# adaLN steps moved out of the first head pair of a neighbourhood-attention stage

## The chip, the cores and the metric

The kernel runs on one core of a Trainium2 chip. The time is device microseconds of one execution; a run is the median of several. The engines are TensorE (PE; PEld is its weight load), VectorE (DVE), ScalarE (ACT), GpSimd (POOL) and SyncE (SP), which here only issues DMAs.

## The reference, cut to what matters

Two layers over 512 latent and 256 context tokens of width 1024: a gated linear attention layer and a neighbourhood attention layer, each followed by a gated MLP with a width-3 convolution. Every sub-layer is RMSNorm, adaLN (a shift and a scale), mixer, gate, residual. The neighbourhood layer, for 16 heads of 64:

```python
mod_l = (sc_lat @ ada_w[i] + ada_b[i])[:, None, :]
sh1_l, s1_l, g1_l, sh2_l, s2_l, g2_l = jnp.split(mod_l, 6, axis=-1)
h_l = modulate(x_lat, norm1_g[i], sh1_l, s1_l)
s_nb = jnp.einsum('bchd,bicjhd->bhcij', q_r, k_win)      # 8 x 16 window of latent keys
s_nb = s_nb + bias[None]                                 # learned, by relative place
s_cx = jnp.einsum('bchd,blhd->bhcl', q_r, k_c)           # all 256 context keys
p = jax.nn.softmax(jnp.concatenate([s_nb, s_cx], axis=-1), axis=-1)
o = p_nb @ v_win + p_cx @ v_c
x_lat = x_lat + g1_l * (o @ w_out)
```

The second layer's MLP uses sh2, s2 and g2 of the same `mod_l`; the context's output is not needed any more.

## The kernel before, in words

**Order of the work.** The program is written with a tile framework. The source gives an order of instructions; a planner then orders each engine's queue, by its own estimate of what is ready when, the earlier in the source first among the ready ones. At run time each engine works its queue strictly in that order, and a wait holds everything behind it on the same engine. SP's queue of DMA issues is such a queue too. A tile pool's memory goes to the next pool when the old pool's users are done.

**Matmuls.** Every weight tile of 128 x 1024 comes by DMA into a `st` tile (three buffers) and is split into a high part (`wh`, ACT, L283) and a rest (`wl`, DVE, L284); a product is three matmuls (`mm3`, L288 to L290). The split weights live in a ring that holds five such tiles.

**Last step of the MLP before.** `last_outs` (L1053) adds the outputs to the residual and runs the next norm along with them, first for the latents, then for the context. The norm's temporary tiles come from `scratch`: `tt`, which is one buffer and listed twice, and four big tiles (3h, 3l, 4h, 4l), in the order tt, 3h, 3l, tt, 4h, 4l. All lie in the pool `ffn0`, whose memory the neighbourhood stage's pool `na` takes over. A norm step writes `hh` (ACT) and `hl` (DVE).

**The neighbourhood stage** goes over eight pairs of heads. For pair `pr` the queries, keys and values were projected during pair `pr - 1` (`proj`, with weights that `weights` loads and splits). The latents are in 4 tiles of 128 tokens. For each tile `t`: `scores(pr, t)` does the score matmuls (L1207), then for each of the two heads DVE adds the bias and takes the row maximum (L1214, `mx`), POOL negates it (L1217, `ng`), ACT takes the exponential and its sum (L1219), DVE the reciprocal (L1221, `ri`), POOL scales the row (L1222, `S`). `turn(pr, t)` transposes the probabilities on PE (L1232) and copies them to `PT`, one head by ACT (L1235), one by DVE (L1237). `values(pr, t)` multiplies with the values (L1249). Between these stand the projections for the next pair, and for odd pairs from 3 on the output projection of two earlier pairs (`out_group`, added to the residual by DVE, L312).

**Bias.** `raw` holds a pair's learned bias, `nmask` two masks (inner and edge), both loaded at the start of the stage, L1126 and L1130. POOL fills the tiles `bias0` and `bias1` with constants and adds raw and mask into their first and last quarter and a half (L1145, four additions per head). Tile 0 reads columns 256 to 768 (edge), the others columns 0 to 512 (inner).

**adaLN.** Four vectors of 1024 (gate 1, shift 2, scale 2, gate 2 of the second layer) are computed on DVE meanwhile: `ada_lanes` makes 33 jobs, one that starts two loads and 8 steps for each vector. A step multiplies a 128 x 1024 tile `sa` with a column and accumulates in `acc` (L206 for the first, L208 for the others), and issues the load for the step after next (L198); `sa` has two buffers. The eighth step also sums `acc` over partitions on PE (L214), turns the result and adds its bias. Each pair takes four jobs from the list, at four places between its scores and transposes.

Of the kernel before, what the change touches and what calls it, by code (L numbers as in the profile page):

```python
# [13 lines left out]
OP = mybir.AluOpType  # L14
# [25 lines left out]
def body(ctx, tc, x, ctx_x, small, ada0, ada, w_gla, a_w1, a_w2, w_go, w_fi, w_fo,  # L40
         w_nqk, w_no, rpb, ident_d, rope_d, lvl_d, nmask_d, *outs):
    nc = tc.nc
# [372 lines left out]
    with tc.tile_pool(name="gla", bufs=6) as pool:  # L415
# [342 lines left out]
        for h in range(HEADS):  # L758
            part_a(h, turn_early if h == HEADS - 1 else None)
            n = h + 1  # L760
# [76 lines left out]
    def ffn0():  # L837
# [3 lines left out]
        with tc.tile_pool(name="ffn0", bufs=1) as pool:  # L841
            def big(i, e, dt=FR):
                return pool.tile([128, 4 * HT], dt, name=f"T{i}{e}", tag=f"T{i}{e}")

            def scratch(tags):

                n = [0]

                def new(name):
                    n[0] += 1  # L850
                    tg = tags[n[0] % len(tags)]
                    if tg == "tt":
                        return pool.tile([128, T + 1], F32, name=name, tag="tt")[:, 0:512]
                    return big(*tg, F32)[:, 0:512]

                return new
# [10 lines left out]
            tmp = scratch([(i, e) for i in (4, 2) for e in "hl"])  # L867
# [96 lines left out]
            def weights_a(j):  # L964

                s_ = st[j] = {"a": wload(w_fi[0, j, 0])}
                s_["A"] = wsplit(s_["a"])
# [15 lines left out]
            def weights_c(j):  # L983
                st[j]["S4"], st[j]["A22"] = (wsplit(t_)[0] for t_ in st[j]["left"])

            def first(j):
                s_ = st[j]
                s_["b1"], s_["b2"] = ps_aux(), ps_mm()
                product(s_["b1"], s_["A"][0], 11, True)
                s_["s1"] = copied(s_["b1"])  # L990
                product(s_["b2"], s_["A"][1], 21, True)
# [27 lines left out]
            def lane():  # L1019
                if jobs:  # L1020
                    jobs.pop(0)()

            jobs = ada_lanes([(1, m, c) for m in range(2) for c in range(2)],
                             lambda: ast.tile([128, 1024], F32, name="acc", tag="sa"),
                             lambda: pool.tile([128, HT], F32, name="rows", tag="cp", bufs=5)[:, 0:256], 1)
# [4 lines left out]
            for grp in GROUPS:  # L1030
                for j in grp:
                    if j < 2:
                        continue
                    if j < NF - 1:
                        weights_a(j + 1)
                    weights_c(j)
                    if j < NF - 1:
                        first(j + 1)
                    us[j] = final_(j)
                    if j < NF - 1:  # L1040
                        to_pad(j + 1)
                        weights_b(j + 1)
                        middle(j + 1)
                ul = [us[j] for j in grp]
                n = len(grp)
                w = [h for j in grp for h in wsplit(wload(w_fo[0, j]))]

                def block(i):
                    return lambda d: tuple(t_[:, d % 4 * 128:d % 4 * 128 + 128] for t_ in w[d // 4 * n + i])

                ws = [block(i) for i in range(n)]
                if grp is GROUPS[-1]:
                    last_outs(0, ws, ul, 0, (LAT, CTX),  # L1053
                              lambda rng: Norm(pool, 1, 0, rng, blocks=rng == LAT, acc=apad[:, rng[0]:rng[1]],
                                               tmp=scratch(["tt", (3, "h"), (3, "l"), "tt", (4, "h"), (4, "l")])))
                    continue
                for d in range(KD):
                    for rng in (LAT, CTX):
                        add_gated(ffn_out(ws, ul, d, rng, 0), 0, 1, d, rng)
# [60 lines left out]
    with tc.tile_pool(name="na", bufs=5) as pool:  # L1120
# [6 lines left out]

        load_raw(0)
        nmask = pool.tile([128, 2, 256], F32, name="nmask", bufs=1)
        nc.sync.dma_start(nmask, nmask_d.rearrange("v p n -> p v n"))  # L1130
        biasT = [pool.tile([128, 768], F32, name=f"bias{i}", bufs=1) for i in range(2)]
        for bt in biasT:
            nc.gpsimd.memset(bt, 0.0)
# [1 line left out]
                nc.gpsimd.memset(bt[0:64, o + 192:o + 256], NEG)  # L1135
                nc.gpsimd.memset(bt[64:128, o:o + 64], NEG)

        def load_bias(hd):
            bt = biasT[hd % 2]
            rv = raws[hd // 2][:, hd % 2, :]  # L1140
            for var, o in ((0, 0), (1, 512)):
                for half in range(2):
                    ps_ = slice(64 * half, 64 * half + 64)
                    o2 = o + 64 * half
                    nc.gpsimd.tensor_tensor(bt[ps_, o2:o2 + 192], rv[ps_], nmask[ps_, var, 64 * half:64 * half + 192],  # L1145
                                            OP.add)
            return bt

        biases = {0: [load_bias(hh) for hh in range(2)]}
        sp = [dict() for _ in range(8)]  # L1150

        def weights(pr, i):
            sp[pr]["w", i] = tuple(w.rearrange("p (k n) -> p k n", k=KD) for w in wunit(w_nqk[pr, i]))
# [46 lines left out]
        def scores(pr, t):  # L1200
            qe, ke = sp[pr][0], sp[pr][1]
            pss = [ps_aux() for _ in range(2)]
            for off, ks in ((W0[t], slice(128 * t, 128 * t + 256)), (C0[t], slice(640, 896))):
                for i, (a_, b_) in enumerate(((1, 0), (0, 1), (0, 0))):
                    for hh in range(2):
                        p_ = slice(64 * hh, 64 * hh + 64)
                        mm(pss[hh][:, off:off + 256], qe[a_][p_, 128 * t:128 * t + 128], ke[b_][p_, ks],  # L1207
                           start=i == 0, stop=i == 2)
            S2 = res.tile([128, D], F32, name="S2", tag="xc", bufs=2)
            for hh in range(2):  # L1210
                S = S2[:, hh * 512:hh * 512 + 512]
                mx = sml.tile([128, 1], F32, name="mx", tag="mx")
                bt = biases[pr][hh]
                nc.vector.tensor_tensor_reduce(S, pss[hh], bt[:, 0:512] if t else bt[:, 256:768], 1.0, -3.0e38,  # L1214
                                               OP.add, OP.max, mx)
                ng = sml.tile([128, 1], F32, name="ng", tag="ng")
                nc.gpsimd.tensor_scalar(ng, mx, -1.0, 0.0, OP.mult, OP.add)  # L1217
                sm = sml.tile([128, 1], F32, name="sm", tag="sm")
                nc.scalar.activation(S, S, AF.Exp, bias=ng, accum_out=sm)  # L1219
                ri = sml.tile([128, 1], F32, name="ri", tag="ri")  # L1220
                nc.vector.reciprocal(ri, sm)  # L1221
                nc.gpsimd.tensor_scalar(S, S, ri, 1.0, OP.mult, OP.mult)  # L1222
            sp[pr]["S", t] = S2

# [47 lines left out]
        def out_groups(m, t0, t1):  # L1272
            for d in range(2 * t0, 2 * t1):
                out_group(m, d)

        jobs = ada_lanes([(1, m, 0) for m in range(2, 6)],
                         lambda: pool.tile([128, 1024], F32, name="acc", tag="acc", bufs=1),
                         lambda: pool.tile([128, 256], F32, name="rows", bufs=1), 2)
        jobs.pop(0)()
        for i in range(3):  # L1280
            weights(0, i)
        for i in range(3):
# [5 lines left out]
        for pr in range(8):  # L1288
            nx = pr + 1
            more = nx < 8  # L1290
            m = (pr - 3) // 2
            outs_now = pr >= 3 and pr % 2 == 1
            if more:
                for i in range(3):
                    weights(nx, i)
            if outs_now:
                out_weights(m)
            if more:
                load_raw(nx)
            scores(pr, 0)  # L1300
            if pr:
                values(pr - 1, 3)
            if more:
                proj(nx, 0, LAT)
            scores(pr, 1)
            if more:
                proj(nx, 1, LAT)
            elif outs_now:
                out_groups(m, 0, 1)
            jobs.pop(0)()  # L1310
            turn(pr, 0)
            scores(pr, 2)
            jobs.pop(0)()
            values(pr, 0)
            if more:
                proj(nx, 1, CTX)
                proj(nx, 2, CTX)
                v_turn(nx, CTX)
            if outs_now:
                out_groups(m, 1 - more, 2)  # L1320
            turn(pr, 1)
            scores(pr, 3)
            jobs.pop(0)()
            values(pr, 1)
            if more:
                biases[nx] = [load_bias(2 * nx + hh) for hh in range(2)]
                proj(nx, 2, LAT)
            turn(pr, 2)
            jobs.pop(0)()
            if outs_now:  # L1330
                out_group(m, 4)
                if more:
                    out_group(m, 5)
            if more:
                v_turn(nx, LAT)
            values(pr, 2)
            turn(pr, 3)
            if outs_now and more:
                out_groups(m, 3, 4)
# [118 lines left out]
```

## Time and profile before

| | |
|---|---|
| median of 3 runs | 1719.58 us (1718.56 to 1719.92) |
| profiled execution | 1717.33 us |
| its span, first to last instruction | 1715.5 us |
| PE busy | 1647.6 us, 96% |
| DVE busy | 1188.4 us, 69% |
| ACT busy | 740.0 us, 43% |
| POOL busy | 205.8 us, 12% |
| share of PE in the chain that ended last | 73% |
| neighbourhood stage | about 994 to 1318 us of the span |

A busy PE is not PE at its peak, as matmuls overlap; what counts is where it stops, for whom, and at which granted clock. All times in the rows are from the span's start.

### The profile page before, as it was taken

The numbers are of one execution on the slowest core, as the hardware profiler recorded it, in microseconds if no ns is written. First come the engines' busy times: TensorE is split into PE (matmuls) and PEld (weight loads), VectorE is DVE, ScalarE is ACT, GpSimd is POOL, SyncE is SP. The second block draws the span as 40 slices with busy tenths as digits, with TensorE's granted clock in tenths as the row PEclk, the third lists the DMA queues.
The fourth block names the chain that finished last, engine by engine and source line by source line (L and its number), as shares of the span: only waits on it lengthen the run. The fifth ranks groups of instructions, "written<-read, shape, count | busy, mean of one in ns | idle before, by whom it ended". The sixth has DMA issues, their size and how long they took to land.

```text
span 1715.5 us, 27141 instructions
## 1 busy us (share of the span) xinstructions
PE 1647.6 (96%) x10867; PEld 1413.3 (82%) x10867; DVE 1188.4 (69%) x1973; ACT 740.0 (43%) x1331; POOL 205.8 (12%) x321
## 2 busy tenths in 40 slices
PE   5999999999999999999999989999999999999997
PEld 3768778777899999999999768887877888888887
DVE  4797877875998877978767774647476755555555
ACT  3665756663753342433434544433334522222332
POOL 1031222320000000000000042423231000000000
PEclk9999999999999999999999989999999999999999
DMA  7653423013333332524223151414141232322321
GB/s 270 182 173 106 166 75 105 20 50 136 98 122 112 116 106 75 172 67 143 98 63 110 27 191 54 141 47 161 41 135 38 85 96 90 99 89 84 110 86 50
DMA packets 54190, 179.70 MB, mean 105 GB/s; under 512 B 7024, under 2 KB 10864, under 8 KB 54064
## 3 DMA queue, kind: packets, MB, share of 16 engines
q1 hardware_dynamic: 54064, 177.97, 32.4%
q8 instruction: 85, 1.39, 0.3%
q14 instruction: 41, 0.34, 0.1%
HBM read 173.75 MB, written 2.10 MB: 103 GB/s over the span
## 4 chain that ended last, share of the span: by engine, by line
PE 73%; DVE 11%; ACT 5%; issue 4%; POOL 3%; DMA 3%; SPq 0%; POOLq 0%; DVEq 0%; ACTq 0%
PE mm L288 14%; PE mm L289 14%; PE mm L290 14%; PE aux L288 8%; PE aux L289 8%; PE aux L290 8%; PE mm L1249 1%; DMA sa<-in 1%; PE aux L1232 1%; POOL bias L1145 1%; DVE t L571 1%; DVE acc L208 1%; PE aux L650 1%; PE aux L1207 1%; PE aux L615 1%
## 5 line engine op out<-in xcount | busy, mean ns | idle before, releaser
L288 PE MATMUL mm<-hh,wl 128*128 128x512 f32 (+3 forms) x864 | 308.1, 359 | 5.0 <-ACT hh L372 2.5
L289 PE MATMUL mm<-hl,wh 128*128 128x512 f32 (+3 forms) x864 | 302.9, 351 | 0.0
L290 PE MATMUL mm<-hh,wh 128*128 128x512 f32 (+3 forms) x864 | 302.4, 351 | 0.0
L289 PE MATMUL mm<-ul,wh 128*128 128x512 f32 (+1 forms) x544 | 188.7, 347 | 0.2 <-DVE ul L301 0.2
L288 PE MATMUL mm<-uh,wl 128*128 128x512 f32 (+1 forms) x544 | 188.9, 349 | 0.0
L290 PE MATMUL mm<-uh,wh 128*128 128x512 f32 (+1 forms) x544 | 188.7, 348 | 0.0
L288 PEld LDWEIGHTS mm<-hh,wl 128*128 128x128 f32 (+1 forms) x864 | 163.7, 190 | 29.0 <-issue 5.3
L312 DVE SCALAR_TENSOR_TENSOR xl<-mm,mod,xl 128x512 f32<-128x512 f32 (+1 forms) x168 | 116.2, 698 | 94.4 <-PE mm L290 93.8
L283 ACT ACTIVATE wh<-st 128x1024 fp32r<-128x1024 f32 (+1 forms) x127 | 131.8, 1051 | 113.5 <-issue 69.6
L290 PEld LDWEIGHTS mm<-hh,wh 128*128 128x128 f32 (+1 forms) x864 | 164.0, 190 | 18.0 <-issue 0.4
L289 PEld LDWEIGHTS mm<-hl,wh 128*128 128x128 f32 (+1 forms) x864 | 164.1, 190 | 17.7 <-issue 1.0
L288 PE MATMUL aux<-hh,wl 128*128 128x384 f32 (+2 forms) x496 | 173.9, 351 | 0.0
L289 PE MATMUL aux<-hl,wh 128*128 128x384 f32 (+2 forms) x496 | 173.5, 350 | 0.0
L290 PE MATMUL aux<-hh,wh 128*128 128x384 f32 (+2 forms) x496 | 173.4, 350 | 0.0
L284 DVE TENSOR_TENSOR wl<-st,wh 128x1024 fp32r<-128x1024 f32 (+1 forms) x126 | 153.8, 1226 | 22.5 <-ACT wh L283 22.1
L263 ACT ACTIVATE wh<-st 128x512 fp32r<-128x512 f32 (+1 forms) x126 | 94.1, 756 | 165.0 <-issue 57.0
L348 POOL TENSOR_TENSOR rs<-ms,mhalf 128x2 f32<-128x2 f32 (+1 forms) x10 | 10.9, 1094 | 932.2 <-DVE ms L346 932.2
L288 PEld LDWEIGHTS mm<-uh,wl 128*128 128x128 f32 x544 | 102.4, 189 | 15.9 <-ACT uh L300 2.0
L289 PEld LDWEIGHTS mm<-ul,wh 128*128 128x128 f32 x544 | 102.5, 188 | 15.0 <-DVE ul L301 0.6
L264 DVE TENSOR_TENSOR wl<-st,wh 128x512 fp32r<-128x512 f32 (+1 forms) x126 | 104.6, 849 | 13.6 <-ACT wh L263 13.0
L290 PEld LDWEIGHTS mm<-uh,wh 128*128 128x128 f32 x544 | 102.4, 188 | 13.2
L288 PEld LDWEIGHTS aux<-hh,wl 128*128 128x128 f32 x496 | 93.6, 189 | 8.5 <-issue 1.2
(330 smaller groups left out, 3251.3 us busy)
## 6 DMA issues: line engine op xcount, KB each, us to landing
st<-in SPq DMA_DIRECT2D x201, 512.0 KB, 3.7
sa<-in SPq DMA_DIRECT2D x98, 512.0 KB, 4.2
sx<-in SPq DMA_DIRECT2D x14, 512.0 KB, 6.1
xl<-in SPq DMA_DIRECT2D x8, 512.0 KB, 6.2
xc<-in SPq DMA_DIRECT2D x4, 512.0 KB, 8.2
out<-y SPq DMA_DIRECT2D x16, 128.0 KB, 1.7
raw<-in SPq DMA_DIRECT2D x16, 96.0 KB, 2.4
t<-q SPq DMA_DIRECT2D x16, 64.0 KB, 2.5
```

Source lines behind the costliest of these rows:

```text
L208: nc.vector.scalar_tensor_tensor(acc[0], st, cs[:, k, c:c + 1], acc[0], OP.mult, OP.add)
L263: nc.scalar.activation(hi, s_, AF.Copy)
L264: nc.vector.tensor_sub(lo, s_, hi.bitcast(F32))
L283: nc.scalar.activation(hi, st, AF.Copy)
L284: (eng or nc.vector).tensor_sub(lo, st, hi.bitcast(F32))
L288: mm(out, a[1], b[0], start=first, stop=False, **at)
L289: mm(out, a[0], b[1], start=False, stop=False, **at)
L290: mm(out, a[0], b[0], start=False, stop=last, **at)
L312: nc.vector.scalar_tensor_tensor(x_, ps, gate(l, n, d, rng), x_, OP.mult, OP.add)
L571: nc.vector.tensor_mul(ek, ek, st[h]["k"])
L615: mm(ps[:, 0:DV], st[h]["kt", d][:, c * CH:(c + 1) * CH], st[h]["v", c], start=True, stop=True)
L650: mm(ps[:, 0:DV], a_, b_, start=i == 0, stop=i == len(terms) - 1)
```

## The change

The neighbourhood stage takes no adaLN job in pair 0; pairs 1 to 4 take five, pairs 5 to 7 four. Each job's DVE instructions are queued on DVE behind the last softmax reciprocal written before it (`tc.issue_after` fixes the order on one engine's queue and adds no wait for an end). The weight loads of the next pairs are queued on SP behind the load of the mask. The bias additions go edge first, both heads, then inner, both heads. The norm at the end of the MLP before no longer uses `tt` as a scratch tile.

```diff
-                                               tmp=scratch(["tt", (3, "h"), (3, "l"), "tt", (4, "h"), (4, "l")])))
+                                               tmp=scratch([(3, "h"), (3, "l"), (4, "h"), (4, "l")])))
...
-        nc.sync.dma_start(nmask, nmask_d.rearrange("v p n -> p v n"))
+        mask_load = nc.sync.dma_start(nmask, nmask_d.rearrange("v p n -> p v n"))
...
-        def load_bias(hd):
-            bt = biasT[hd % 2]
+        def bias_part(hd, var, o):
             rv = raws[hd // 2][:, hd % 2, :]
-            for var, o in ((0, 0), (1, 512)):
-                for half in range(2):
...
+        def load_biases(pr):
+            for var, o in ((1, 512), (0, 0)):
+                for hh in range(2):
+                    bias_part(2 * pr + hh, var, o)
...
-                nc.vector.reciprocal(ri, sm)
+                anchor[0] = nc.vector.reciprocal(ri, sm).ins
...
+        def lane(pr, fifth=False):
+            if pr and (pr < 5 or not fifth):
+                with tc.issue_after(anchor[0]):
+                    jobs.pop(0)()
...
             if more:
-                for i in range(3):
-                    weights(nx, i)
+                with tc.issue_after(mask_load.ins):
+                    for i in range(3):
+                        weights(nx, i)
...
                 proj(nx, 0, LAT)
+            lane(pr, fifth=True)
             scores(pr, 1)
...
-            jobs.pop(0)()
+            lane(pr)
             turn(pr, 0)
             scores(pr, 2)
-            jobs.pop(0)()
+            lane(pr)
             values(pr, 0)
...
             scores(pr, 3)
-            jobs.pop(0)()
+            lane(pr)
             values(pr, 1)
             if more:
-                biases[nx] = [load_bias(2 * nx + hh) for hh in range(2)]
+                load_biases(nx)
                 proj(nx, 2, LAT)
             turn(pr, 2)
-            jobs.pop(0)()
+            lane(pr)
```

## Rows read from the trace of the kernel before

**Rows 1.** Waits of PE, first pair, 1002 to 1036 (total us, times, longest).

```profile
PE mm L1249 <- DVE PT L1237: 2.5, 1, 2.5
PE mm L1249 <- ACT PT L1235: 2.3, 1, 2.3
...
PE aux L1232 <- POOL S L1222: 0.9, 1, 0.9
```

**Rows 2.** Waits of PE, later pairs, 1036 to 1320.

```profile
PE mm L1249 <- DVE PT L1237: 3.8, 3, 2.1
```

**Rows 3.** Timeline of PE, first pair (start, duration, instruction, count).

```profile
1014.45 0.60 PE L1232 MATMUL aux<-ident,S 128*128 128x128 f32 x4
...
1026.56 0.58 PE L288 MATMUL mm<-hh,wl 128*128 128x256 f32 x1
...
1030.55 0.28 PE L288 MATMUL mm<-hh,wl 128*128 128x256 f32 x1
...
1034.13 0.40 PE L288 MATMUL mm<-hh,wl 128*128 128x512 f32 x1
...
1035.10 1.04 PE L1232 MATMUL aux<-ident,S 128*128 128x128 f32 x8
...
1038.00 0.50 PE L288 MATMUL mm<-hh,wl 128*128 128x512 f32 x1
```

**Rows 4.** Stretches: us; busy PE, PEld, DVE, ACT, POOL; granted clock, DMA share, GB/s.

```profile
1020.50:1026.50 6.00, 2.52 (x16) 1.85 (x16) 5.58 (x9) 1.75 (x6) 2.11 (x3) 0.50 0.69 207
1026.50:1030.50 4.00, 4.00 (x19) 3.94 (x19) 0.41 (x4) 1.31 (x4) 1.57 (x3) 0.50 0.23 91
```

**Rows 5.** Timeline of DVE, first pair (idle before, and what ended it, in brackets).

```profile
1013.78 1.28 DVE L208 SCALAR_TENSOR_TENSOR acc<-sa,cs,acc 128x1024 f32<-128x1024 f32 x1 [4.47 <-DMA sa<-in]
...
1020.90 2.91 DVE L208 SCALAR_TENSOR_TENSOR acc<-sa,cs,acc 128x1024 f32<-128x1024 f32 x2
...
1023.94 0.68 DVE L1237 COPY PT<-aux 128x512 f32<-128x512 f32 x1
```

**Rows 6.** Stretches, adaLN accumulation alone: busy PE, PEld, DVE; clock, DMA share, GB/s.

```profile
993.00:1030.00 37.00, 0.00 (x0) 0.00 (x0) 10.93 (x8) 0.87 0.61 194
1030.00:1079.00 49.00, 0.00 (x0) 0.00 (x0) 0.00 (x0) 0.99 0.16 52
...
1243.00:1272.00 29.00, 0.64 (x8) 0.16 (x8) 10.47 (x8) 1.00 0.58 181
```

**Rows 7.** Timeline of POOL, first pair.

```profile
1000.12 7.21 POOL L1145 TENSOR_TENSOR bias<-raw,nmask 64x192 f32<-64x192 f32 x8 [2.89 <-DMA nmask<-in]
...
1011.31 0.70 POOL L1222 TENSOR_SCALAR S<-S,ri 128x512 f32<-128x512 f32 x1
...
1021.08 1.66 POOL L1222 TENSOR_SCALAR S<-S,ri 128x512 f32<-128x512 f32 x1 [0.33 <-DVE ri L1221]
```

**Rows 8.** Timeline of DVE, seventh pair.

```profile
1268.84 1.29 DVE L208 SCALAR_TENSOR_TENSOR acc<-sa,cs,acc 128x1024 f32<-128x1024 f32 x1 [0.63 <-DMA sa<-in]
```

**Rows 9.** DMA issues (KB, us to landing): whole page, then 993 to 1003.

```profile
st<-in SPq DMA_DIRECT2D x201, 512.0 KB, 3.7
...
nmask<-in SPq DMA_DIRECT2D x1, 256.0 KB, 4.9
```

**Rows 10.** Timeline of SP's DMA queue, 970 to 1012.

```profile
977.93 15.86 SPq L247 DMA_DIRECT2D st<-in  x5
993.89 1.17 SPq L1126 DMA_DIRECT2D raw<-in  x2
995.11 0.58 SPq L1130 DMA_DIRECT2D nmask<-in  x1
```

**Rows 11.** Timeline of DVE, end of the norm before the stage.

```profile
992.17 1.22 DVE L284 TENSOR_TENSOR wl<-st,wh 128x1024 fp32r<-128x1024 f32 x1
993.31 0.48 DVE L373 SCALAR_TENSOR_TENSOR hl<-hf,mod,hh 128x256 fp32r<-128x256 f32 x1
```

**Rows 12.** Timeline of PE, entry of the stage.

```profile
994.76 0.39 PE L288 MATMUL mm<-hh,wl 128*128 128x256 f32 x1 [1.39 <-ACT v L1171]
```

More of the change, by code (lines that the diff above doesn't have):

```diff
@@ L1136, in body @@
                 nc.gpsimd.memset(bt[64:128, o:o + 64], NEG)
-        def load_bias(hd):
-            bt = biasT[hd % 2]
+        def bias_part(hd, var, o):
             rv = raws[hd // 2][:, hd % 2, :]
-            for var, o in ((0, 0), (1, 512)):
-                for half in range(2):
[L1143 to L1149, printed above, removed]
+            for half in range(2):
+                ps_ = slice(64 * half, 64 * half + 64)
+                o2 = o + 64 * half
+                nc.gpsimd.tensor_tensor(biasT[hd % 2][ps_, o2:o2 + 192], rv[ps_],
+                                        nmask[ps_, var, 64 * half:64 * half + 192], OP.add)
+        def load_biases(pr):
+            for var, o in ((1, 512), (0, 0)):
+                for hh in range(2):
+                    bias_part(2 * pr + hh, var, o)
+        load_biases(0)
         sp = [dict() for _ in range(8)]
@@ L1212, in scores @@
                 mx = sml.tile([128, 1], F32, name="mx", tag="mx")
-                bt = biases[pr][hh]
+                bt = biasT[hh]
                 nc.vector.tensor_tensor_reduce(S, pss[hh], bt[:, 0:512] if t else bt[:, 256:768], 1.0, -3.0e38,
@@ L1279, in body @@
         jobs.pop(0)()
+        anchor = [None]
+        def lane(pr, fifth=False):
+            if pr and (pr < 5 or not fifth):
+                with tc.issue_after(anchor[0]):
+                    jobs.pop(0)()
         for i in range(3):
```

## The prediction

> **What bounds the kernel now.** The order of reading: who TensorE (PE) waited for, the PE timeline where it waited, then the queue that kept it waiting. In the neighbourhood stage (about 994 to 1318 us of the span) PE nearly always has matmuls, so only its stops are worth time. With the first pair of heads it stopped for both copies of the transposed probabilities, 2.5 and 2.3 us [rows 1]; for all seven later pairs together it waited 3.8 us for such a copy [rows 2]. So the stage has one bad place and three small ones.
>
> The bad place: the transposes of the first pair start at 1014.45, and the next projection, which needs nothing from them, only at 1026.56 because PE works in order behind them [rows 3]. From 1020.5 to 1030.5 the granted clock is 0.50, the lower level, 1.2 GHz, after PE had begun to stop [rows 4].
>
> Why: VectorE (DVE) also works in order. The adaLN accumulation of 1013.78 starts after 4.47 us in which DVE sat idle for that step's DMA; the second head's reciprocal and all later softmax work stand behind it. At 1020.90 two more accumulations (2.91 us) stand ahead of the PT copy of 1023.94 [rows 5]. The code asks for four adaLN jobs per pair, but the planner issues what it thinks ready: all 8 steps of a vector come in one burst (8 in 993 to 1030, none in 1030 to 1079, 8 again in 1243 to 1272) [rows 6]. A burst runs as fast as 512 KB loads land, and softmax shares its queue.
>
> **Part 1: no adaLN step with the first pair.** From the table of jobs: before 8 pairs x 4 = 32 steps; after 0 + 4 x 5 + 3 x 4 = 32. Nothing is removed but the place. Time without stops, from the same pair's second round: transposes at 1035.10, scores, values, next projection at 1038.00, so 2.90 us for the three [rows 3]. From 1014.45 that gives 1017.35 in place of 1026.56: 9.21 us. Then the clock: 18 matmuls of 256 columns took 1026.56 to 1030.55, 3.99 us; the next 30 took 3.58 us (to 1034.13), 0.12 each [rows 3], so 18 cost 2.16: another 1.83 us. Sum 11.04. I take 0.3 off for a remaining wait on a PT copy: **10.7 us**. What is late next? The softmax must be ready at 1014.45 without the accumulations: its POOL work waited behind eight bias additions (1000.12, 7.21 us) and even so the first scaling ran at 1011.31 [rows 7]; the second head's would follow by about 0.7. Cover: the two projections that PE runs until 1014.45. Their weights must then be there (part 3).
>
> **Part 2: later steps pinned behind a softmax's reciprocal.** The 32 steps (about 1.3 us each, 10.2 to 10.9 us for eight [rows 6]) can't run early in bursts any more; each follows the last reciprocal traced before it. Queued behind a pinned step: PT and V copies, key and query splits, the next softmax. Gain: the 3.8 us of [rows 2], where a step with a late load (1268.84, 0.63 idle and 1.29 us) stands just ahead of a PT copy [rows 8]. With one step per softmax two loads are always in flight a softmax apart, longer than the 4.9 us that a load took in a crowd [rows 9]. Bounds: all 3.8 won; or, if a step still lands ahead of each of those three copies, 1.29 lost at each, -3.9. The pin's reason and the free DVE time between bursts put me near the first: **3.0 us**. The fifth jobs in pairs 1 to 4 add 4 x 1.3 = 5.2 us of DVE to stretches that hold no accumulation now [rows 6]: nothing on the path while spread, and 1.29 apiece if ahead of a copy (inside the bound above).
>
> **Part 3: mask, raw bias and the weights of pair 1.** SP issued five weight loads from 977.93 on, then raw at 993.89 and mask at 995.11 [rows 10]. Raw starts 0.1 us after the last `hl` of the context norm ends (993.31 + 0.48), and that norm is the last user of the previous pool [rows 11]. So mask and raw wait for the pool, not for SP, and taking `tt` out of the scratch list cannot by itself release them: the same last norm step writes another tile of that pool. What can: pair 1's weight loads now stand behind the mask, so their two DVE splits (like that of 992.17, 1.22 us, 1.14 until the next starts) no longer stand among the norm's steps. That moves the release to about 993.8 - 2.3 = 991.5, mask to 992.7. PE's idle 1.39 us at 994.76, waiting for the evacuation that waits for the same release [rows 12], may go too: gain 0 to 1.4. Price: pair 1's first weights are issued after the mask, at about 993.4 instead of 977.93; plus 3.7 (median landing) to 4.9 us [rows 9], plus the two halves of a split, about 2.3 (each near the 1.22 of the DVE half): usable 999.4 to 1000.6, or up to 2.3 us later if the release isn't earlier (1002.9). PE takes them after two context projections of 24 matmuls (48 x 0.12 = 5.8 us) and the first scores (about 1.5, half of the 2.90 above): 994.76 + 7.3 = 1002.1, or 1000.7 if the 1.4 is gained. So between -1.5 and +1.4 us; the nearest case is just in time: **+0.6 us gained**.
>
> Scratch of four tiles for one `tt` and four: every step now waits for the fourth before it, instead of `tt` for the third. DVE was busy nearly without a break there, so I count 0, bounds -1.0 to +0.5 (one norm step of 0.48 us, late twice, or early once). Edge biases first: pair 0's first softmax needs four of the eight additions, 3.6 of 7.21 us; nothing waits for it before 1014.45, so 0 now; if the mask came late they are the cover.
>
> **Sum**: 10.7 + 3.0 + 0.6 = 14.3 us. The profiled execution took 1717.33 us, 1.8 around its span of 1715.5; it becomes 1703.0. The median of the runs is 2.25 above the profiled one: 1719.58 - 14.3 = **1705.3 us**.
>
> **A rule against the change.** POOL's scaling of the probabilities took 0.70 us at 1011.31 and 1.66 at 1021.08, where it started just after an accumulation [rows 5, 7]. The pin puts every accumulation right behind the reciprocal that releases such a scaling. The Trainium skill (SBUF — State Buffer, Who interferes with whom) says that a DVE instruction with two SBUF inputs and a GpSimd instruction that reads SBUF exclude each other for the whole instruction, whoever starts first. By that rule, and the trace agrees with it here, each scaling beside a step would be about 1 us later; the sum would be unchanged as long as PE has a projection between softmax and transposes.
>
> **Rivals.**
> A. The stall only moves: part 1 comes, part 2 doesn't, and pairs 2, 4 and 6 keep their stops or trade them for others of 1.29 us per step; entrance 0. For it: DVE is dense there. Against: only three steps must miss a copy. 10.7 - 2.0 = 8.7 gained (between 10.7 and 6.8): **1710.9**.
> B. Mask no sooner, weights of pair 1 late (the part that doesn't do what it says). The pool is released at 993.8 still; weights usable 1002.9 to 1005 (the second of them a step behind the first), PE stops 1 to 3 us before its projection and may fall to the lower clock for another 1.8, as in the first pair. 10.7 + 3.0 - 4.8 = 8.9: **1710.7**. For it: the release is by the last norm step in both kernels.
> C. No change: the first pair's stop is not DVE's. If, with accumulations gone, the PT copies were as late, only part 2's 3 us would come and the weights' delay would eat them: **1719**. Against it: the 4.47 us idle is named DMA of `sa`, and that DMA is gone.
> D. Slower: the collision of scaling and accumulation reaches PE. Place: POOL's scaling after each pinned step; price 1.66 - 0.70 = 0.96 us each; up to 32 steps, 31 us. It cancels the gain from 14.3 / 0.96 = 15 steps on; at 25 of 32 (24 us): 1719.58 - 14.3 + 24 = **1729**. Against it: PE waited for a scaling once, 0.9 us, and inside the bad place [rows 1]; between any scores and their transposes stand at least two groups of projection, as from 1002 to 1014.45.
>
> **How the numbers follow.** Forecast 0.62 (own range 1701.5 to 1709), A 0.13, B 0.12, C 0.07, D 0.06. 0.2% (3.4 us) is about what a measurement of this kernel can tell from no change. Forecast, A and B are faster: 0.87, with a little of C's lower side against a little of A's upper one. C is the same: 0.07. D slower: 0.06. The range reaches from 1701.5 (all of 11.0, 3.8, 1.4 and 0.5, and the 1.4 by which the runs shown differ) to 1713 (A and B with their worse ends), leaving out C, D and thin tails.
>
> **What would show it.** Right: no accumulation before about 1040; the transposes of the first pair followed without a stop by scores, values and projection at about 1016 to 1018; granted clock 1.00 through 1014 to 1034; one accumulation behind each second reciprocal afterwards; the waits for PT in later pairs under 1 us. Part 3 right: mask issued at about 992.7 and no PE stop at the first pair-1 projection; wrong: mask still near 994 or PE waiting for `wl` at about 1001. The prediction is wrong if the first pair still stops PE for more than 3 us, or if scalings beside accumulations are what PE's transposes wait for.

## The result, and the profile after

The changed kernel takes **1704.18 us**, median of 5 runs (1703.84 to 1705.13), against 1719.58 (1718.56 to 1720.27, 5 runs): a ratio of 0.9910, 95% interval [0.9899, 0.9921]. That is 15.4 us faster; forecast were 14.3 and 1705.3 us. The profiled execution took 1703.84 us, its span 1702.1. Of the five executions behind run 8's 1702.91 us below, one took 5473.84 us at a granted clock of 0.269, and it is the profiled one, so no row of that run is shown.

Who PE waited for, 1002 to 1320 of the changed kernel, the window of [rows 1, 2] together (total us, times, longest):

```profile
PE mm L288 <- DVE xl L312: 2.0, 1, 2.0
PE mm L288 <- DVE wl L284: 1.7, 1, 1.7
PE mm L288 <- ACT oh L300: 0.9, 1, 0.9
PE mm L1252 <- DVE PT L1240: 0.7, 1, 0.7
PE aux L214 <- DVE acc L208: 0.5, 1, 0.5
```

The lines after L1055 have moved by a few (L1249 is L1252 now, L1237 is L1240, L1222 is L1225). Both waits of [rows 1] for copies of PT are gone, and so are the three of [rows 2]. The 0.7 us for PT are new: they stand in pair 7, behind a pinned step, where before no accumulation ran (PE and DVE after; accumulations alone before):

```profile
1285.00 1.09 PE L1252 MATMUL mm<-PT,V 128*64 128x128 f32 x14 [0.69 <-DVE PT L1240]
```

```profile
1283.08 1.26 DVE L208 SCALAR_TENSOR_TENSOR acc<-sa,cs,acc 128x1024 f32<-128x1024 f32 x1
```

```profile
1272.00:1318.00 46.00, 0.64 (x8) 0.16 (x8) 0.00 (x0) 1.00 0.08 24
```

The wait for `wl` is new too (part 3 below); the two for `xl` and `oh` lie at the stage's end and were there before (1.7 and 0.7 us).

The first pair on PE, in answer to [rows 3] (start, duration, instruction, count):

```profile
1015.60 1.03 PE L1235 MATMUL aux<-ident,S 128*128 128x128 f32 x8
...
1016.56 0.39 PE L1210 MATMUL aux<-kh,ql 64*128 64x256 f32 x2
...
1017.47 1.09 PE L1252 MATMUL mm<-PT,V 128*64 128x128 f32 x16
1018.49 0.39 PE L288 MATMUL mm<-hh,wl 128*128 128x256 f32 x1
```

Transposes, scores, values, next projection, without a stop: 2.89 us from 1015.60 to 1018.49, where before it took 12.11 (1014.45 to 1026.56). The stretches, in answer to [rows 4] (us; busy PE, PEld, DVE, ACT, POOL; granted clock, DMA share, GB/s):

```profile
1015.60:1021.00 5.40, 5.40 (x58) 4.92 (x57) 3.31 (x10) 3.32 (x9) 2.40 (x6) 1.00 0.33 100
1021.00:1037.00 16.00, 16.00 (x128) 13.53 (x126) 6.83 (x13) 6.18 (x12) 4.62 (x9) 1.00 0.15 46
```

The granted clock stays at 1.00, its upper level, where it was 0.50. The accumulations alone, in answer to [rows 6] (busy PE, PEld, DVE; clock, DMA share, GB/s):

```profile
993.00:1030.00 37.00, 0.00 (x0) 0.00 (x0) 0.00 (x0) 1.00 0.51 166
1030.00:1079.00 49.00, 0.00 (x0) 0.00 (x0) 7.69 (x6) 1.00 0.34 106
1079.00:1104.00 25.00, 0.64 (x8) 0.19 (x8) 2.85 (x3) 1.00 0.33 107
1104.00:1158.00 54.00, 0.00 (x0) 0.00 (x0) 8.89 (x7) 1.00 0.38 115
```

0, 6, 3, 7 where [rows 6] show bursts of 8 and nothing between. One pinned step at work on DVE (start, duration, instruction, count):

```profile
1050.29 0.16 DVE L1224 RECIPROCAL ri<-sm 128x1 f32<-128x1 f32 x1 [0.54 <-ACT S L1222]
1050.37 1.31 DVE L208 SCALAR_TENSOR_TENSOR acc<-sa,cs,acc 128x1024 f32<-128x1024 f32 x1
...
1052.30 0.69 DVE L1240 COPY PT<-aux 128x512 f32<-128x512 f32 x1 [0.27 <-PE aux L1235]
```

The step sits behind the second head's reciprocal and is over before the copy of PT is due: the copy waits for PE, not PE for the copy. The 32 steps stand behind 25 softmaxes. 18 stand alone; the last two of each of pairs 1 to 7 stand together behind the pair's last softmax, as the source writes both jobs behind the same reciprocal. So in pair 1:

```profile
1066.50 2.97 DVE L208 SCALAR_TENSOR_TENSOR acc<-sa,cs,acc 128x1024 f32<-128x1024 f32 x2
```

The entrance, in answer to [rows 10 to 12]: SP's queue, then DVE's last norm step, then PE:

```profile
992.16 1.18 SPq L1126 DMA_DIRECT2D raw<-in  x2
993.39 0.58 SPq L1130 DMA_DIRECT2D nmask<-in  x1
994.01 1.42 SPq L247 DMA_DIRECT2D st<-in  x3
```

```profile
991.59 0.48 DVE L373 SCALAR_TENSOR_TENSOR hl<-T4l,mod,hh 128x256 fp32r<-128x256 f32 x1
```

```profile
994.03 0.36 PE L288 MATMUL mm<-hh,wl 128*128 128x256 f32 x1 [0.24 <-DVE ql L1186]
...
1002.11 0.50 PE L288 MATMUL mm<-hh,wl 128*128 128x512 f32 x1 [1.67 <-DVE wl L284]
```

Raw still starts 0.1 us after the norm's last `hl`. PE's stop of 1.39 us [rows 12] has become 0.24, and a stop of 1.67 us stands at 1002.11, at pair 1's first weights. Their loads landed late (DMA issues of 993.9 to 995.6; KB, us to landing):

```profile
st<-in SPq DMA_DIRECT2D x3, 512.0 KB, 6.5
```

The sum by place. As work upstream of the change also differs a little from one execution to the next, the count starts at the first residual addition of the MLP's last step (DVE L312, 943.92 before, 945.51 after):

| us between | before | after | gained | forecast |
|---|---|---|---|---|
| that addition and the first scores of pair 0 (entrance) | 58.14 | 57.71 | 0.4 | 0.6 |
| first scores of pair 0 and of pair 1 (first pair) | 44.83 | 33.91 | 10.9 | 10.7 |
| first scores of pair 1 and of pair 7 | 243.71 | 238.51 | 5.2 | 3.0, with the next line |
| first scores of pair 7 and the end | 124.93 | 126.41 | -1.5 | |
| sum | | | 15.1 | 14.3 |

### The profile page after: what moved, and what is told of

It reads as the page before. It is cut to its first block, busy times and chain, and to the rows that moved or that the text cites. A ratio compares the mean times of both kernels' runs of the same rounds, so it can differ in the third digit from the quotient of the medians.

```text
span 1702.1 us, 27128 instructions
## 1 busy us (share of the span) xinstructions
PE 1643.6 (97%) x10867; PEld 1409.3 (83%) x10867; DVE 1190.5 (70%) x1973; ACT 740.5 (44%) x1331; POOL 217.4 (13%) x321
## 3 DMA queue, kind: packets, MB, share of 16 engines
q8 instruction: 85, 1.39, 0.3%
## 4 chain that ended last, share of the span: by engine, by line
PE 79%; DVE 10%; ACT 5%; issue 2%; DMA 2%; POOL 2%; SPq 0%; POOLq 0%; ACTq 0%; DVEq 0%
PE mm L288 16%; PE mm L290 15%; PE mm L289 15%; PE aux L288 8%; PE aux L289 8%; PE aux L290 8%; PE mm L1252 2%; PE aux L1235 2%; PE aux L1210 2%; DMA st<-in 1%; DVE t L571 1%; PE aux L650 1%; PE aux L615 1%; ACT wh L283 1%; DVE t L570 1%
## 5 line engine op out<-in xcount | busy, mean ns | idle before, releaser
L312 DVE SCALAR_TENSOR_TENSOR xl<-mm,mod,xl 128x512 f32<-128x512 f32 (+1 forms) x168 | 116.1, 697 | 96.2 <-PE mm L290 95.8
```

The costliest lines, as they stand in the source:

```text
L312: nc.vector.scalar_tensor_tensor(x_, ps, gate(l, n, d, rng), x_, OP.mult, OP.add)
```

## The experiments

The theory to test: adaLN steps bunched by the planner ahead of the softmax on DVE's in-order queue made PE stop, by their wait for loads and by their own time; the pin spreads them, and spread they are hidden. Against it stood: that mask and bias did it, that an empty first pair did it, and that POOL's scaling would take the gain back. Ratios are to the kernel before, run beside.

**1. The adaLN move alone.** In the kernel before only:

```diff
+                anchor[0] = nc.vector.reciprocal(ri, sm).ins
...
+        def lane(pr, fifth=False):
+            if pr and (pr < 5 or not fifth):
+                with tc.issue_after(anchor[0]):
+                    jobs.pop(0)()
...
-            jobs.pop(0)()
+            lane(pr)
```

> Only the adaLN steps move (none with pair 0, five in pairs 1 to 4, each pinned behind a reciprocal); mask, raw bias, weight order and scratch as before. Theory (bursts of adaLN on DVE's queue were the stall): parts 1 and 2 of the prediction, 10.7 + 3.0 = 13.7 us below before, so about 1706, and within 2 us of the changed kernel; no PE stop over 0.6 us between 1014 and 1021, clock 1.00 there. Rival (the softmax of pair 0 was late because mask and bias came late, POOL's eight additions ahead of it): gain at most 4 us, about 1716, and a stop of over 4 us stays at the first pair's transposes or values.

Measured: 1705.02 us, ratio 0.9908 [0.9892, 0.9924]. From the first scores of pair 0 to those of pair 7 PE's times are the changed kernel's within 0.1 us (first pair 33.91, pairs 1 to 7 238.58). The entrance takes 58.79, with the old stops:

```profile
PE mm L288 <- ACT v L1171: 1.4, 1, 1.4
PE aux L351 <- POOL rs L348: 1.2, 1, 1.2
```

(PE's waits from 978 to 1010 of this run.) The mask goes out 51.9 us after the L312 of the table, 47.9 in the changed kernel. The move is the whole gain; the late mask costs it nothing in the first pair.

**2. The rest alone.** The changed kernel with four unpinned jobs in every pair:

```diff
-            lane(pr, fifth=True)
...
-            lane(pr)
+            jobs.pop(0)()
```

> The complement: mask and raw bias sooner, edge first, weights behind the mask, scratch without tt, but adaLN's 32 steps in the old places and unpinned. Theory: the bursts come back, pair 0 stops PE for about 9 us and the clock falls; the rest is worth part 3's 0.6 us (-1.5 to +1.4), so 1718 to 1721. Rival (the earlier mask is what helps pair 0): 1712 or less, with the first transposes followed by projections before 1020.

Measured: 1716.23 us, ratio 0.9973 [0.9961, 0.9984], 4.6 us faster: 1.8 us better than the theory's range and 4.2 short of the rival's, so neither held. The first pair takes 37.96 us, 6.9 less than before, the later ones 246.07, 2.4 more. The stop is smaller, and DVE in the first pair of this run shows what is different:

```profile
1008.18 3.00 DVE L208 SCALAR_TENSOR_TENSOR acc<-sa,cs,acc 128x1024 f32<-128x1024 f32 x2
1011.10 0.15 DVE L1224 RECIPROCAL ri<-sm 128x1 f32<-128x1 f32 x1
1012.11 0.17 DVE L1224 RECIPROCAL ri<-sm 128x1 f32<-128x1 f32 x1 [0.86 <-ACT S L1222]
```

The burst is there, but the planner laid the queue out anew (the weights' splits moved), and no step that waits for its load stands between the two reciprocals, as the one of [rows 5] with 4.47 us does. So the effects don't add: where the steps burst, what else is moved shifts where they fall; with the steps pinned the rest is worth what the entrance shows. Whether the sooner mask has a part in this order no run tells; with the steps pinned it is worth nothing in the first pair (run 1).

**3. The pin taken away**, the table of jobs kept:

```diff
-                with tc.issue_after(anchor[0]):
-                    jobs.pop(0)()
+                jobs.pop(0)()
```

> The changed kernel with the table of jobs kept (source order: none in pair 0) but without the pin. Theory A (the pin is what places the steps; without it the planner pulls the first vector's steps forward into pair 0): at least 6 accumulations before 1030, a stop of several us in pair 0, the time 1714 to 1720. Rival (the place in the source is enough): no accumulation before 1030 and 1704 to 1707.

Measured: 1714.71 us, ratio 0.9959 [0.9943, 0.9975], some 10 us above the changed kernel. Accumulations alone, as above:

```profile
993.00:1030.00 37.00, 0.00 (x0) 0.00 (x0) 9.21 (x7) 1.00 0.72 235
```

Seven before 1030, though the source has none before pair 1: the planner pulls them forward, and the first pair takes 40.69 us, 6.8 more than with the pin. From the first scores of pair 1 to those of pair 7 it takes 244.82 us, 6.3 more: the pin earns both parts.

**4. Pinned, in all eight pairs, four each:**

```diff
-            if pr and (pr < 5 or not fifth):
-                with tc.issue_after(anchor[0]):
-                    jobs.pop(0)()
+            with tc.issue_after(anchor[0]):
+                jobs.pop(0)()
```

> Pinned steps in all eight pairs, four each, pair 0 too; everything else as in the changed kernel. Theory A (it was the bunching ahead of the softmax, not adaLN in pair 0 as such): three or four single accumulations before 1037, each behind a reciprocal; PE waits in pair 0 at most 2.6 us more (two steps of 1.29 ahead of a copy); 1704 to 1707. Rival (pair 0 has no room for any step: its loads are late because 512 KB tiles of weights land at the same time): a stop of over 4 us and the lower clock return, 1712 to 1718.

Measured: 1705.60 us, ratio 0.9910 [0.9895, 0.9925]: the changed kernel's ratio. Steps in the first pair, DVE's timeline of 1010 to 1036:

```profile
1017.94 0.74 DVE L206 TENSOR_SCALAR acc<-sa,cs 128x1024 f32<-128x1024 f32 x1
1022.79 1.27 DVE L208 SCALAR_TENSOR_TENSOR acc<-sa,cs,acc 128x1024 f32<-128x1024 f32 x1
1032.92 2.97 DVE L208 SCALAR_TENSOR_TENSOR acc<-sa,cs,acc 128x1024 f32<-128x1024 f32 x2
```

The first pair takes 34.39 us with four steps in it, the last two behind one reciprocal, 0.5 more than with none. The empty first pair is not what counts; the pin is.

**5. Bursts without their loads.** The kernel before, the steps reading two tiles loaded once (the other 30 loads are left out):

```diff
-            st = sts.pop(i)
+            st = sts[i % ahead] if resident else sts.pop(i)
...
-            load(i + ahead)
+            resident or load(i + ahead)
```

> The kernel before, bursts and all, but the 32 accumulations read two tiles loaded once at the start of the stage (the other 30 loads are left out, and with them the right products). Theory (half the stall is DVE waiting in order for a load, 4.47 and 0.25 us idle in the first pair, half is the steps' own time ahead of softmax and copies): eight accumulations still before 1030, PE stops for 3 to 6 us in the first pair instead of about 9, 1712 to 1716. Rival 1 (only the loads matter): no stop, 1705 to 1708. Rival 2 (only DVE's own time matters): 1718 to 1721.

Measured: 1713.75 us, ratio 0.9966 [0.9951, 0.9981], in the theory's range. The first pair takes 39.24 us. PE's waits in it, 1003 to 1037:

```profile
PE mm L1249 <- ACT PT L1235: 2.3, 1, 2.3
PE aux L1232 <- POOL S L1222: 0.8, 1, 0.8
```

and DVE ahead of them, without any idle time for a load:

```profile
1010.41 2.82 DVE L208 SCALAR_TENSOR_TENSOR acc<-sa,cs,acc 128x1024 f32<-128x1024 f32 x2
1013.15 0.15 DVE L1221 RECIPROCAL ri<-sm 128x1 f32<-128x1 f32 x1
```

44.83 - 39.24 = 5.6 us of the first pair's loss go with the loads, 39.24 - 33.91 = 5.3 stay with the steps' own time. Some 0.9 of the 5.6 is the clock: behind the stop 9 matmuls of the next projection ran 0.21 us apart here and 18 before, the others 0.12. (The planner's order differs a little here too, so the halves are rough.)

**6. Two instructions per step.** In the changed kernel, behind every accumulation but each vector's first:

```diff
+                if twice:
+                    nc.vector.scalar_tensor_tensor(acc[0], st, 0.0, acc[0], OP.mult, OP.add)
```

> The changed kernel with a second vector instruction of the same shape behind every accumulation but each vector's first (a product by zero added to acc): 28 more of about 1.3 us on DVE, 36 us, all pinned behind a reciprocal. Theory (DVE has room when the steps are spread, and a collision with the scaling isn't on PE's path): 1704 to 1708; at most three copies of PT are late by one more step, 3 x 1.29. Rival D (scaling and accumulation collide on PE's path): every step costs a further 0.33 to 0.96 us, 9 to 27 us slower, and PE waits for the scaled S.

Measured: 1723.12 us, ratio 1.0007 [0.9992, 1.0022]: 18.9 us above the changed kernel (16.7 by the two ratios). My 1704 to 1708 was wrong. In the profiled executions 2.7 us of it lie ahead of pair 1, where this kernel has no accumulation: PE's stop for `wl` was 2.8 us long in this execution and the clock fell behind it (last section). 16.2 lie from pair 1 on. The size is rival D's; the place is not. PE's waits, 1036 to 1320:

```profile
PE mm L1254 <- DVE PT L1242: 8.0, 10, 1.5
PE aux L216 <- DVE acc L210: 3.1, 3, 1.8
PE aux L216 <- DVE ql L1188: 1.5, 1, 1.5
```

All that PE waits for is on DVE, but for 0.2 us (a copy of PT on ACT), and nothing is the scaled S. POOL's scalings took hardly longer than in the changed kernel (groups of 1030 to 1310, before, after, this run: busy us, mean ns | idle before):

```profile
L1222 POOL TENSOR_SCALAR S<-S,ri 128x512 f32<-128x512 f32 x58 | 47.4, 825 | 12.5 <-DVE ri L1221 10.5 <-PE aux L1232 0.4
```

```profile
L1225 POOL TENSOR_SCALAR S<-S,ri 128x512 f32<-128x512 f32 x58 | 66.9, 1159 | 11.6 <-DVE ri L1224 9.8 <-PE aux L1235 0.4
```

```profile
L1227 POOL TENSOR_SCALAR S<-S,ri 128x512 f32<-128x512 f32 x57 | 67.9, 1198 | 11.7 <-DVE ri L1226 10.3
```

**7. The second instruction with one input**, to tell DVE's queue from the collision (against run 6's kernel):

```diff
-                    nc.vector.scalar_tensor_tensor(acc[0], st, 0.0, acc[0], OP.mult, OP.add)
+                    nc.vector.tensor_scalar(acc[0], acc[0], 1.0, None, OP.mult)
```

> As the run with every accumulation doubled, but the second instruction has one SBUF input (acc times 1.0, written back) in place of two. Theory (the 19 us of the doubled run are DVE's own queue: a second 1.3 us ahead of the copies of PT): again 12 us or more slower than the changed kernel where the instruction's time is again about 1.3 us, with waits for PT and no wait for S; if it is shorter, less in proportion. Rival (the two-input instruction shuts GpSimd's scaling out, and that is what costs): the scaling's mean falls back towards 0.8 us and the time to 1704 to 1708 even at 1.3 us each.

Measured: 1713.27 us, ratio 0.9957 [0.9943, 0.9971], 9.1 us above the changed kernel (8.1 by the two ratios); in the profiled executions 8.9 us lie from pair 1 on. The added group, 1037 to 1310 (busy us, mean ns | idle before), and PE's first wait of 1036 to 1320:

```profile
L210 DVE TENSOR_SCALAR acc<-acc 128x1024 f32<-128x1024 f32 x28 | 25.8, 922 | 0.8
```

```profile
PE mm L1254 <- DVE PT L1242: 3.6, 4, 1.0
```

The added instructions take 25.8 us in all and cost 8.9; those of run 6 take 41.0 and cost 16.2: 0.34 and 0.39 of the time added to DVE's queue, which these intervals can't tell apart. The scalings add up to 66.5 us here, as in the changed kernel, so it is DVE's queue and not POOL that costs. The scalings have a part in it by lengthening that queue, 0.4 us for some of the added instructions (last section), 7 of the 41 and of the 26 us; what they cost POOL reaches no wait.

Where the price arises shows best behind the second softmax of pair 1. The first value matmuls after it, in the changed kernel, in this run and in run 6, and the added instruction in this run:

```profile
1053.10 1.09 PE L1252 MATMUL mm<-PT,V 128*64 128x128 f32 x16
```

```profile
1052.48 1.63 PE L1254 MATMUL mm<-PT,V 128*64 128x128 f32 x16
```

```profile
1054.83 0.43 PE L1254 MATMUL mm<-PT,V 128*64 128x128 f32 x2
1055.89 1.09 PE L1254 MATMUL mm<-PT,V 128*64 128x128 f32 x14 [0.63 <-DVE PT L1242]
```

```profile
1051.10 1.07 DVE L210 TENSOR_SCALAR acc<-acc 128x1024 f32<-128x1024 f32 x1
```

PE takes 1.09, 1.63 and 2.15 us there, with 1.31, 2.38 and 2.91 us of accumulation (1.31 and the added 1.07 or 1.60) ahead of the copy. 2.38 less the 0.54 lost, and 2.91 less the 1.06 lost, give the same: an estimate of 1.85 us that are free on DVE at this place. One step fits, a step and a further instruction don't.

**8. Fewer steps.** The changed kernel with only the first and last accumulation of each vector (24 of 32 steps and their loads left out):

```diff
+            if few and 0 < k < KD - 1:
+                return
...
-            load(i + ahead)
+            load(i + (8 if few else ahead))
```

> The changed kernel with only the first and the last of each vector's eight accumulations and their loads (the other six products are left out, 24 of 32 steps). Theory (one pinned step per softmax is hidden altogether): 1702 to 1705, the same as the changed kernel within 2 us, though DVE does 31 us and POOL's scaling about 15 us less. Rival (each pinned step costs PE a little too, as the doubled ones cost 0.5 us each): 24 x 0.2 to 0.5 us, 1692 to 1699.

Measured: 1702.91 us, ratio 0.9898 [0.9874, 0.9923], not to be told from the changed kernel's 0.9910 [0.9899, 0.9921]. 24 x 1.36 us of DVE leave, and the median falls by 1.3 us; the intervals alone would allow some 6. The changed kernel's own trace says the same: behind its steps PE stops for 0.7 us (PT) and 0.5 (`acc`), 1.2 in all. So the pinned steps are nearly hidden, the single ones and the two behind a pair's last softmax.

**9. Parts of the entrance.** The weights pin, `tt`, and the pin for two of the three weight tiles only:

```diff
-                with tc.issue_after(mask_load.ins):
-                    for i in range(3):
-                        weights(nx, i)
+                for i in range(3):
+                    weights(nx, i)
```

> The changed kernel with the weights of the next pairs not held behind the mask. Theory (part 3 is an exchange: 1.83 us of stop for late weights in place of 1.36 + 1.55 us of stops before): PE's stop for wl at about 1002 goes, the release of the pool comes 2 to 3 us later again and the stop of about 1.4 us for the evacuation behind it comes back; time within 2 us of the changed kernel, 1703 to 1706, pair 0 untouched. Rival B of the prediction (the late weights are a net loss): 1.8 us faster, about 1702.4, with no stop over 0.6 us in their place.

```diff
-                                               tmp=scratch([(3, "h"), (3, "l"), (4, "h"), (4, "l")])))
+                                               tmp=scratch(["tt", (3, "h"), (3, "l"), "tt", (4, "h"), (4, "l")])))
```

> The changed kernel with the two tt entries back in the scratch list of the norm. Theory (0, bounds -0.5 to +1.0 for the step): 1703.5 to 1705.5; the mask goes out within 0.5 us of the same time. Rival (tt is what held the pool, and its removal what released mask and raw): mask about 2 us later, the biases with it, and 1 to 2 us slower.

```diff
+                weights(nx, 0)
                 with tc.issue_after(mask_load.ins):
-                    for i in range(3):
+                    for i in range(1, 3):
```

> The changed kernel with only the first of the three weight tiles of the next pair free to go before the mask, the other two behind it as before. Theory (the stop of 1.83 us at 1002 is the first weight tile's load and split, and one split ahead of the norm's end delays the release by about 1.1 us, which PE has no use for until its context projection): the stop goes, up to 1.4 us returns at the context projection; 1702.5 to 1704.5. Rival (each split ahead of the norm is worth what it costs): 1704 to 1705, no change.

| | us | ratio, interval | mask issued after that L312 | PE's stops in the entrance, us |
|---|---|---|---|---|
| before | | | 51.2 | v 1.4, rs 1.2, wl 0.2 |
| changed | 1704.18 | 0.9910 [0.9899, 0.9921] | 47.9 | wl 1.7, hl 0.4, ql 0.2, hh 0.2 |
| weights free | 1703.38 | 0.9897 [0.9871, 0.9924] | 50.8 | v 0.7, hh 0.7, rs 0.6, wl 0.2 |
| tt back | 1706.77 | 0.9915 [0.9892, 0.9938] | 48.5 | rs 1.2, wl 1.0 |
| first weight free | 1705.20 | 0.9908 [0.9884, 0.9932] | 50.3 | v 1.8, hh 0.7, rs 0.6, ql 0.3, wl 0.2 |

The weights' pin moves the mask by 2.9 us, taking `tt` out by 0.6, and no variant can be told from the changed kernel: each trades one stop for others. The last one's expected gain did not come: its stop of 1.8 us for `v`, an evacuation on ACT, took the place of the one for `wl`. The run with `tt` back came out above its expected 1703.5 to 1705.5 and scatters (1703.59 to 1709.78); its ratio doesn't differ from the changed kernel's. The edge-first order was not run by itself; with the rest it is worth nothing that shows.

## Why the prediction was right, and where its steps were not

**What bounds the kernel: right.** The first pair's stop was DVE's queue, with bursts ahead of softmax and copies; runs 1, 3, 4 and 5 show it from four sides. Run 2 fits it only with the new order of its queue, which was not foreseen. The split that [rows 5] suggest, a wait for a load and then the steps' own time, measured 5.6 and 5.3 us.

**Part 1: size right (10.9 for 10.7), reason half wrong.** It was costed as "no adaLN step with the first pair". Run 3 has none there in the source and seven on the chip; run 4 has four there and loses 0.5 us. What removes the burst is the pin, named only in part 2. The step that would have shown it stood in the prediction itself: the code asked for four jobs per pair and the planner issued eight at once, so a new place in the source alone couldn't be trusted to hold. The rest of the working held: 2.89 us without a stop (2.90 taken from the second round), clock 1.00 and no half-clock stretch, nothing new late.

**Part 2: right in sum, by two errors that cancel.** Forecast were 3.0, bounds -3.9 and 3.8; measured are 5.2 between pairs 1 and 7 and -1.5 behind them, 3.7 together. The 5.2 is above the upper bound, which counted PE's stops alone: these fell from 4.0 to 0.6 us (PE's idle time between the two places), and the value matmuls around a stop, too, took longer than without one (PE busy 239.7 before, 237.9 after). The loss behind was not forecast at all: pair 7 had no accumulation and has four now, and half of the 1.5 us is the stop of 0.69 us for PT behind the first of them; the other half is open. That the two nearly meet the 3.0 is luck. Wrong, too, is "one step per softmax" in the argument on loads: seven of the 25 softmaxes carry two. It did no harm, as the pair behind the last softmax is hidden as well, but the margin is narrow: a further instruction behind each step is not free (runs 6, 7).

**Part 3: release right, cover wrong.** The mask went out 3.3 us sooner, mainly by the pin of the weights (2.9, worked out as 2.3), with 0.6 from `tt`, which was counted as nothing; the release still came with the norm's last step. But by the prediction's own sign, PE waiting for `wl` at about 1001, the second half failed: pair 1's weights were late by 1.7 us. The term that was too small is the landing, 3.7 to 4.9 us forecast and 6.5 measured for the three loads issued together. The cover was too long as well: PE wanted these weights ahead of the first scores and not behind them, at 1000.4 (1002.11 less the stop). The stop ate most of what was won at the two others (1.4 and 1.2). The gain of 0.4 for 0.6 shows nothing: the changed kernel and runs 4, 6 and 7, whose source is the same up to there, took 57.71, 57.89, 58.89 and 59.53 us for the entrance.

**The rule against the change held, and its effect too.** Scalings beside an accumulation took longer: the mean of all rose from 0.83 to 1.16 us, 19.5 us more of POOL in all, and PE waited for none of them (0.9 before). The sum is unchanged, as a projection stands between softmax and transposes. By the rule of the Trainium skill (SBUF — State Buffer, Who interferes with whom), two-input DVE instructions and GpSimd's reads exclude each other; the 66.9 against 47.4 us agree.

**The rivals.** A fell (the stops of [rows 2] are gone, 0.7 us in pair 7 is new), C fell with the first pair. B's late weights came, at 1.7 us, but the release was sooner too. D's price came on POOL and not on PE. The gain can be lost by another way, as run 6 shows, which is no faster than the kernel before: by DVE's own queue, with an added instruction behind nearly every step.

## What to carry to other kernels

Where a planner orders an in-order queue, read from the trace where side work really stands, not from the source: eight steps meant for two pairs stood in one, ahead of the softmax. Pin each step behind the last instruction that the critical path needs from that engine, and then test the margin by adding to it: here the steps cost 1.2 us of stops in all, and more work behind each cost a third to two fifths of its time, as about 1.85 us were free at the place that was measured and a step took 1.31. Look also at the places that had no side work before: spread out, the steps reached pair 7, where one cost a stop. A release that opens sooner because something else was queued behind it gives back what that something then is late; count both ends.

## What the runs showed of the hardware that was not expected

POOL's scaling holds up DVE too, where it started first. The instructions added in run 6 (count, least, median and longest ns):

```profile
L210 DVE SCALAR_TENSOR_TENSOR acc<-sa,acc x28: 1207/1598/1603, 1053.4 to 1315.3; 128x1024 f32<-128x1024 f32 x28
```

The 18 of 28 that took 1.60 us are those that began with a scaling under way for another 0.53 us; the others, among them two in which a scaling began 0.1 us after them, took 1.21. The one-input instruction of run 7 did the same, 1.07 us against 0.68 without a scaling.

The granted clock did not follow the length of one stop. Stops of 1.7 us in the changed kernel and 1.9 in run 4, both for `wl` at the stage's entrance, left it at 1.00, the upper level; with one of 2.8 us there in run 6 part of the time behind it was at the lower level, and with one of 1.8 us in the last run of 9 too (us; busy PE to POOL; clock, DMA share, GB/s; run 4, run 6, last run of 9):

```profile
1002.00:1008.00 6.00, 4.34 (x27) 3.48 (x28) 5.30 (x8) 3.23 (x5) 2.61 (x4) 1.00 0.45 144
```

```profile
1002.00:1006.00 4.00, 3.72 (x20) 2.95 (x21) 3.83 (x7) 1.65 (x4) 0.15 (x1) 0.71 0.68 194
```

```profile
1002.00:1008.00 6.00, 4.22 (x24) 3.04 (x24) 4.60 (x8) 5.01 (x6) 3.21 (x6) 0.86 0.50 148
```

What else decides it these rows don't tell.
